# Seven half-size products in two chunks of the half-GLU, and merged rows added by transfers

## The chip, the cores and the metric

The kernel runs on one core of a Trainium2 chip. The core has a matrix engine (TensorE, in the profile PE for its matmuls and PEld for its weight loads), a vector engine (VectorE, DVE), an engine for activations (ScalarE, ACT), a general one (GpSimd, POOL) and one that here only issues transfers (SyncE, SP). They share an on-chip memory of 128 partitions (SBUF); matmuls write to a second, small one (PSUM). Each engine works through its own list of instructions in order and waits for others on semaphores. Transfers (DMA) are issued by SP, ACT or POOL, and those of one issuer form a queue.

The metric is the device time of one execution in microseconds (us). The kernel before takes 1742.87 us, the median of three executions from 1741.56 to 1743.77.

## The reference

One layer of a hybrid encoder, in fp32, applied to two requests of 256 and 512 tokens with the same weights. Three mixers (an S5 state-space model, differential attention, attention into memory tokens) work on the same projection of the input; then come the parts that this case is about:

```python
z = jax.nn.gelu(y)
s5_out = z * jax.nn.sigmoid(z @ s5_w_glu)                  # half-GLU
...
branches = jnp.stack([s5_out, diff_out, mem_out], axis=2)
br = jnp.einsum('blnc,ncd->blnd', branches, w_branch)      # three 1024 x 1024 products
gates = jax.nn.sigmoid(gl + b_gate)
merged = jnp.sum(gates * br, axis=2)
x = x + merged @ w_out
```

A feed-forward layer follows. z has 1024 channels for 768 tokens (both requests side by side); `s5_w_glu`, each `w_branch` and `w_out` are 1024×1024.

## The kernel before

**Products.** Activations lie with channels on partitions: eight rows of 128 channels × 768 tokens. An fp32 product is made of three matmuls of a shortened format (`mm3`): weights and activations are each split into a high and a low part, and high·high, high·low and low·high are added in PSUM. In the profile these are lines L755, L756 and L757. A 1024×1024 weight matrix is worked in four chunks of 256 columns. A chunk by the plain way takes, for each of two 128-column halves, eight k-steps of three matmuls over 256 tokens and three over 512: 96 matmuls.

**Seven products.** The last of the three branch products (`w_branch1`, function `branch7`) is made by a Strassen scheme with Winograd's sums. A chunk's weights are seen as four blocks: A11, A21 (the first 512 input channels, for the two output halves) and A12, A22 (the other 512). The activations are four blocks too: B11, B12 (first 512 channels, tokens 0–383 and 384–767) and B21, B22. Instead of eight block products there are seven: A11·B11, A12·B21, S1·T1, S2·T2, S3·T3, S4·B22 and A22·T4, with S1 to S4 sums of weight blocks and T1 to T4 differences of activation blocks. Each takes 4 k-steps × 3 = 12 matmuls over 384 tokens, so a chunk has 84. A11·B11, S2·T2 and S3·T3 add up in one PSUM tile (`chain`, name `brc`); after each of them ACT copies the tile out (c11, c12, c21: L1683, L1685, L1690) before the next may add to it. S4·B22 is added to S1·T1's tile (`p5`), which ACT has copied to c22 (L1687). DVE adds the other products to these quarters (`plus`, L1673).

**Weights** come through `WStream`: SP loads two tiles of 512 KB a chunk; for a plain chunk ACT makes the high part (L599) and DVE the low part (L605), each 128×1024. For a chunk of kind `w2`, POOL makes S1, S2, S3, S4 (L574, L575, L581, L583, in two buffers), and each of the seven factors, 128×512, is split by ACT (L557) and DVE (L558). The split tiles have four buffers, in which two factors share a tile.

**Order of the stages.** Branch 2 (memory attention), the half-GLU of the S5 branch in four plain chunks (L1590 to L1613), preparation of the T blocks for the last branch, branch 0 (S5), branch 1 by `branch7`, then `w_out`. The half-GLU computes, for a chunk, tanh of half the product (L1611), then (1+tanh)·z with z loaded again from its copy in DRAM by POOL's queue (`zs`, L1604), then splits the result into high and low (`s5o`, tiles S, lines L749 and L750). z itself stays split in the tiles Z (`zhi`, `zlo`).

**Merging** in `branch7`: a gate row comes from DRAM by POOL's queue (L1657), ACT turns it into tanh (L1658), DVE multiplies it with a result row `cs[m]` (L1677), the product is added to the row of `merged` (L1678; the chunk's first row by POOL, its second by DVE), and `merged` is split for `w_out` into MG (`mgd`: ACT L1679, DVE L1680).

**Buffers.** The pool `stg` has two buffers of 128×768, tag `brr`, which serve the reloaded z rows and, in `branch7`, the two result rows of a chunk (named `bs`). The gates and the GLU's results (`gt`) share two buffers of another pool. PSUM tiles of products have three buffers.

What sets the order on each engine is a planner: the program is written stage by stage, and a scheduler that simulates the engines orders every engine's list by when operands and buffers come free. So matmuls of the next chunk stand between those of the one before, and the written order is not the order run.

## Time and profile before

| | |
|---|---|
| median of three executions | 1742.87 us |
| profiled execution | 1743.06 us |
| its span (first to last instruction) | 1741.3 us |
| PE busy | 1726.6 us, 99% of the span |
| DVE, ACT, POOL busy | 1300.5, 908.6, 302.5 us |
| half-GLU, four chunks | from 987.07 to 1053.89 us |
| preparation and branch 0 | to 1120.74 us |
| last branch (`branch7`) | to 1183.75 us |

A row of the timeline has the start, the duration, the engine, the line, the operation, the tile written and the tiles read, and in brackets how long the engine had been idle before and what ended that. A row of groups has the count behind an x, the busy time, the mean nanoseconds of one, and idle time before them with its releasers. Matmuls overlap, so their pace is the distance between their starts. A row of transfers has the size and the median time from issue to landing.

### The profile page before, as it was taken

To read this page: it belongs to the slowest core of one execution; us is meant where nothing else is said; L and a number is where in the kernel's file an instruction comes from. 1 tells how busy PE (TensorE), PEld (TensorE's weight loads), DVE (VectorE), ACT (ScalarE), POOL (GpSimd) and SP (SyncE) were. 2 spreads that over 40 slices of the span, in tenths; PEclk is the share of its full clock that TensorE was granted. 3 is DMA by queue.
4 is the path that set the end of the run, shared out by engine and by line. 5 is a ranking of instruction groups with operands and counts; after the bars stand their busy time and mean duration, and the time that the engine had idled before them with its cause. 6 is when DMAs were issued, how large, how long until landed. Compare 5 with 4: busy or idle time off the path is not lost.

```text
span 1741.3 us, 29531 instructions
## 1 busy us (share of the span) xinstructions
PE 1726.6 (99%) x11188; PEld 1608.1 (92%) x11188; DVE 1300.5 (75%) x2405; ACT 908.6 (52%) x1924; POOL 302.5 (17%) x308
## 2 busy tenths in 40 slices
PE   9999999999999999999999999999999999999999
PEld 9999988999999999999989888998889999998887
DVE  7665749699999778887886536685598777776775
ACT  7444543776767346877765434353343333334443
POOL 0000000000000100111000001341036555541130
PEclk9999999999999999999999999999999999999999
DMA  7222636755556454745653435335312323239974
GB/s 268 78 85 91 125 120 135 186 125 143 145 159 159 115 140 103 164 91 156 155 165 117 140 116 157 103 111 174 97 55 91 110 91 109 92 110 295 248 157 97
DMA packets 209213, 234.09 MB, mean 134 GB/s; under 512 B 57832, under 2 KB 173296, under 8 KB 209072
## 3 DMA queue, kind: packets, MB, share of 16 engines
q1 hardware_dynamic: 182160, 167.49, 32.0%
q0 software_dynamic: 17440, 58.34, 15.6%
q10 hardware_dynamic: 9472, 6.39, 1.3%
q8 instruction: 88, 1.44, 0.4%
q14 instruction: 53, 0.43, 0.1%
HBM read 165.78 MB, written 41.22 MB: 119 GB/s over the span
## 4 chain that ended last, share of the span: by engine, by line
PE 95%; DVE 2%; ACT 1%; issue 0%; DMA 0%; POOL 0%; SPq 0%; ACTq 0%; DVEq 0%
PE gl L755 4%; PE gl L756 4%; PE gl L757 4%; PE gate L755 3%; PE gate L756 3%; PE up L756 3%; PE gate L757 3%; PE up L755 3%; PE up L757 3%; PE dn L757 3%; PE dn L755 3%; PE dn L756 3%; PE br L755 3%; PE br L757 3%; PE br L756 3%; PE qk L755 3%
## 5 line engine op out<-in xcount | busy, mean ns | idle before, releaser
L599 ACT ACTIVATE wh<-wr 128x1024 fp32r<-128x1024 f32 x116 | 131.9, 1138 | 52.3 <-PE br L756 13.3
L605 DVE TENSOR_TENSOR wl<-wr,wh 128x1024 fp32r<-128x1024 f32 x74 | 99.2, 1342 | 63.5 <-ACT wh L599 61.7
L755 PE MATMUL gl<-H,wh 128*128 128x256 f32 (+1 forms) x384 | 132.2, 344 | 0.0
L757 PE MATMUL gl<-H,wl 128*128 128x256 f32 (+1 forms) x384 | 129.0, 336 | 0.0
L756 PE MATMUL gl<-H,wh 128*128 128x256 f32 (+1 forms) x384 | 128.7, 335 | 0.0
L603 POOL DMA_DIRECT2D wl<-wr x42 | 36.6, 872 | 483.3 <-ACT wl L602 464.1
L755 PE MATMUL qk<-wh,H 128*128 128x256 f32 x384 | 108.3, 282 | 0.0
L756 PE MATMUL qk<-wl,H 128*128 128x256 f32 x384 | 108.0, 281 | 0.0
L757 PE MATMUL qk<-wh,H 128*128 128x256 f32 x384 | 107.3, 279 | 0.0
L558 DVE TENSOR_TENSOR wl_S<-ws,wh_S 128x512 fp32r<-128x512 f32 x84 | 70.7, 863 | 26.2 <-ACT wh_S L557 26.2
L756 PE MATMUL dn<-wld,dxh 128*128 128x512 f32 x231 | 89.6, 389 | 0.0
L755 PE MATMUL dn<-whd,dxh 128*128 128x512 f32 x231 | 89.5, 389 | 0.0
L757 PE MATMUL dn<-whd,dxl 128*128 128x512 f32 x231 | 88.9, 389 | 0.0
L557 ACT ACTIVATE wh_S<-ws 128x512 fp32r<-128x512 f32 x84 | 49.5, 625 | 73.5 <-PE up L756 36.6
L757 PEld LDWEIGHTS gl<-H,wl 128*128 128x128 f32 x384 | 72.0, 188 | 8.1
L756 PEld LDWEIGHTS gl<-H,wh 128*128 128x128 f32 x384 | 72.2, 188 | 7.2
L755 PEld LDWEIGHTS gl<-H,wh 128*128 128x128 f32 x384 | 72.3, 188 | 6.9
L757 PEld LDWEIGHTS qk<-wh,H 128*128 128x128 f32 x384 | 72.6, 189 | 0.6
L755 PEld LDWEIGHTS qk<-wh,H 128*128 128x128 f32 x384 | 72.4, 188 | 0.6
L756 PEld LDWEIGHTS qk<-wl,H 128*128 128x128 f32 x384 | 72.3, 188 | 0.5
L1296 DVE TENSOR_REDUCE nm<-sc 128x1 f32<-128x512 f32 (+1 forms) x96 | 56.7, 597 | 18.1 <-PE sc L1291 17.2
L1298 ACT ACTIVATE p<-sc,nm 128x512 f32<-128x512 f32 (+1 forms) x96 | 58.8, 615 | 14.4 <-DVE nm L1296 13.9
(535 smaller groups left out, 6076.2 us busy)
## 6 DMA issues: line engine op xcount, KB each, us to landing
wr<-in_w_in_dram SPq DMA_DIRECT2D x48, 512.0 KB, 5.0
wr<-in_w_gate_up_dram SPq DMA_DIRECT2D x44, 512.0 KB, 3.6
wl<-wr POOLq DMA_DIRECT2D x42, 512.0 KB, 5.4
wr<-in_w_branch_dram SPq DMA_DIRECT2D x24, 512.0 KB, 4.5
glr<-gl_scr POOLq DMA_DIRECT2D x24, 384.0 KB, 3.5
hid_scr<-fa SPq DMA_DIRECT2D x11, 768.0 KB, 6.4
wr<-in_w_mem_kv_dram SPq DMA_DIRECT2D x16, 512.0 KB, 4.4
wr<-in_w_in_dram SPq DMA_DIRECT2D x32, 256.0 KB, 3.9
```

The source lines that it names most:

```text
L557: self.nc.scalar.activation(f(hi), src, AF.Copy)
L558: self.nc.vector.tensor_tensor(out=f(lo), in0=src, in1=f(hi).bitcast(F32), op=ALU.subtract)
L599: self.nc.scalar.activation(hi, r, AF.Copy)
L603: self.nc.gpsimd.dma_start(lo, r.bitcast(F32R), accum_op=ALU.add)
L605: self.sub.tensor_tensor(out=lo, in0=r, in1=hi.bitcast(F32), op=ALU.subtract)
L755: pe.matmul(ps, wh, xh, start=start, stop=False, **kw)
L756: pe.matmul(ps, wh, xl, start=False, stop=False, **kw)
L757: pe.matmul(ps, wl, xh, start=False, stop=stop, **kw)
L1296: v.tensor_reduce(out=nm[:, m : m + 1], in_=ps, axis=AX.X, op=ALU.max, negate=True)
L1298: act.activation(pm[:, 0:n], ps, AF.Exp, bias=nm[:, m : m + 1], accum_out=s1s[:, tt : tt + 1] if m == 0 else s2)
```

## The change

**Half-GLU.** Chunks 2 and 3 are of kind `w2` and go through a new `glu7`, which makes the seven products with z's blocks. B11, B21 and B22 are slices of Z. T1, T2 and T3 are made by `z_differences`, once for each of the four k-rows while chunks 0 and 1 run: two z rows are loaded again by POOL's queue (into two slots of S that are still free), DVE makes four differences of 128×384, and ACT and DVE split them. T1 lies in S, T2 and T3 in a tile that is otherwise free (`zc`). T4's parts are made when chunk 2 begins, and overwrite Z's block B12, which chunks 2 and 3 don't read. This adds eight loads of 384 KB and, for two chunks, eight weight sums on POOL. POOL's two sum buffers are opened ahead of the half-GLU now. Results go to two tiles `gt` of 128×768 in quarters; tanh, the product with z and the split are done for a quarter at a time (`fin`).

**Last branch.** In chunks 0 to 2 the product of gate and result is added to `merged` by a transfer of POOL's queue that adds at its destination (`accum_op`), in place of the POOL and DVE additions; the split of these two rows into MG (`merged_parts`) stands in the next chunk. In chunk 3 both rows are added by DVE. S1·T1 is written third, ahead of S2·T2.

```diff
     for nme in ("w_branch2", "s5_w_glu", "w_branch0", "w_branch1"):
         for c in range(4):
-            W.add(cols(nme, 256 * c), 8, 256, "w2" if nme == "w_branch1" else None)
+            seven = nme == "w_branch1" or nme == "s5_w_glu" and c > 1
+            W.add(cols(nme, 256 * c), 8, 256, "w2" if seven else None)
...
+        def put(P, n_, k, src, scale=None):
+            split_evac(P[n_][0][:, k], P[n_][1][:, k], src, scale)
+        def prod(w, P, l, r, ps=None, start=True):
+            if ps is None:
+                ps = psd("p7")[:, 0:HT]
+            (wh, wl), (xh, xl) = w[l], P[r]
+            for k in range(4):
+                mm3(ps, wh[:, k], wl[:, k], xh[:, k], xl[:, k], start and k == 0, k == 3, not start)
+            return ps
+        def plus(o, ps):
+            v.tensor_tensor(out=o, in0=o, in1=ps, op=add)
+        def differences(P, k, r0, r1, t4):
+            (b11, b12), (b21, b22) = ((r[:, h1], r[:, h2]) for r in (r0, r1))
+            v.tensor_tensor(out=b11, in0=b12, in1=b11, op=sub)
+            v.tensor_tensor(out=b12, in0=b22, in1=b12, op=sub)
+            v.tensor_tensor(out=b22, in0=b22, in1=b11, op=sub)
+            v.tensor_tensor(out=t4, in0=b21, in1=b22, op=sub)
+            put(P, "T2", k, b22)
+            put(P, "T1", k, b11)
+            put(P, "T3", k, b12)
+        zc = xp.tile([128, 8, TOK], F32R, name="zc", tag="x1")
+        q = quarters(zc)
+        ZB = {"B11": tuple(x[:, 0:4, h1] for x in Z), "B21": tuple(x[:, 4:8, h1] for x in Z),
+              "B22": tuple(x[:, 4:8, h2] for x in Z), "T2": (q[0], q[1]), "T3": (q[2], q[3]),
+              "T1": tuple(halves(x[:, 6:8]) for x in S), "T4": tuple(x[:, 0:4, h2] for x in Z)}
+        zt4 = t4p.tile([128, 4, HT], F32, name="zt4", tag="t4")
+        def z_differences(k):
+            r0, r1 = (S[j][:, 4 + k % 2].bitcast(F32) for j in range(2))
+            gp.dma_start(r0, z_scr[k])
+            gp.dma_start(r1, z_scr[k + 4])
+            (b11, b12), (b21, b22) = ((r[:, h1], r[:, h2]) for r in (r0, r1))
+            d = stg.tile([128, TOK], F32, name=uid("zd"), tag="brr")
+            t1, t3 = d[:, h1], d[:, h2]
+            v.tensor_tensor(out=t1, in0=b12, in1=b11, op=sub)
+            v.tensor_tensor(out=t3, in0=b22, in1=b12, op=sub)
+            put(ZB, "T1", k, t1, 0.5)
+            put(ZB, "T3", k, t3, 0.5)
+            v.tensor_tensor(out=t1, in0=b22, in1=t1, op=sub)
+            v.tensor_tensor(out=zt4[:, k], in0=b21, in1=t1, op=sub)
+            put(ZB, "T2", k, t1, 0.5)
+        def z_row(M):
+            zs = stg.tile([128, TOK], F32, name=uid("zs"), tag="brr")
+            gp.dma_start(zs, z_scr[M])
+            return zs
+        def glu7(c):
+            w = W.get()
+            if c == 2:
+                for k in range(4):
+                    put(ZB, "T4", k, zt4[:, k], 0.5)
+            ts = [gtp.tile([128, TOK], F32, name=uid("gt"), tag="glr") for _ in range(2)]
+            zs = [z_row(2 * c + m) for m in range(2)]
+            (c11, c12), (c21, c22) = ((t[:, h1], t[:, h2]) for t in ts)
+            chain = env.psb("gluc")[:, 0:HT]
+            def fin(m, h):
+                t, M = ts[m][:, h], 2 * c + m
+                act.activation(t, t, AF.Tanh, scale=0.5)
+                v.scalar_tensor_tensor(out=t, in0=t, scalar=1.0, in1=zs[m][:, h], op0=add, op1=mul)
+                split_evac(S[0][:, M, h], S[1][:, M, h], t, 0.25)
+            act.activation(c11, prod(w, ZB, "A11", "B11", chain), AF.Copy)
+            plus(c11, prod(w, ZB, "A12", "B21"))
+            p5 = prod(w, ZB, "S1", "T1")
+            act.activation(c22, p5, AF.Copy)
+            act.activation(c12, prod(w, ZB, "S2", "T2", chain, False), AF.Copy)
+            fin(0, h1)
+            prod(w, ZB, "S3", "T3", chain, False)
+            plus(c22, chain)
+            act.activation(c21, chain, AF.Copy)
+            fin(1, h2)
+            plus(c12, prod(w, ZB, "S4", "B22", p5, False))
+            fin(0, h2)
+            plus(c21, prod(w, ZB, "A22", "T4"))
+            fin(1, h1)
...
+        for c in range(2):
...
+                z_differences(M)
+        for c in range(2, 4):
+            glu7(c)
+        t4 = t4p.tile([128, 4, HT], F32, name="t4", tag="t4")
...
+        def merged_parts(M):
+            act.activation(MG[0][:, M], merged[:, M], AF.Copy, scale=0.5)
+            v.scalar_tensor_tensor(out=MG[1][:, M], in0=merged[:, M], scalar=0.5,
+                                   in1=MG[0][:, M].bitcast(F32), op0=mul, op1=sub)
...
                 def merge(m):
                     M = 2 * c + m
                     v.scalar_tensor_tensor(out=cs[m], in0=gs[m], scalar=1.0, in1=cs[m], op0=add, op1=mul)
-                    (v if m else gp).tensor_tensor(out=merged[:, M], in0=merged[:, M], in1=cs[m], op=add)
-                    act.activation(MG[0][:, M], merged[:, M], AF.Copy, scale=0.5)
-                    v.scalar_tensor_tensor(out=MG[1][:, M], in0=merged[:, M], scalar=0.5,
-                                           in1=MG[0][:, M].bitcast(F32), op0=mul, op1=sub)
-
-                act.activation(c11, prod("A11", "B11", chain), AF.Copy)
-                plus(c11, prod("A12", "B21"))
-                act.activation(c12, prod("S2", "T2", chain, False), AF.Copy)
-                p5 = prod("S1", "T1")
+                    if c < 3:
+                        gp.dma_start(merged[:, M], cs[m], accum_op=add)
+                    else:
+                        v.tensor_tensor(out=merged[:, M], in0=merged[:, M], in1=cs[m], op=add)
+                        merged_parts(M)
+
+                act.activation(c11, prod(w, RB, "A11", "B11", chain), AF.Copy)
+                plus(c11, prod(w, RB, "A12", "B21"))
+                p5 = prod(w, RB, "S1", "T1")
                 act.activation(c22, p5, AF.Copy)
-                prod("S3", "T3", chain, False)
+                act.activation(c12, prod(w, RB, "S2", "T2", chain, False), AF.Copy)
+                prod(w, RB, "S3", "T3", chain, False)
                 plus(c22, chain)
                 act.activation(c21, chain, AF.Copy)
+                if c:
+                    for m in range(2):
+                        merged_parts(2 * c - 2 + m)
                 if c < 3:
-                    plus(c12, prod("S4", "B22", p5, False))
+                    plus(c12, prod(w, RB, "S4", "B22", p5, False))
                     merge(0)
-                    plus(c21, prod("A22", "T4"))
+                    plus(c21, prod(w, RB, "A22", "T4"))
                     merge(1)
                 else:
-                    plus(c21, prod("A22", "T4"))
+                    plus(c21, prod(w, RB, "A22", "T4"))
                     merge(1)
-                    plus(c12, prod("S4", "B22", p5, False))
+                    plus(c12, prod(w, RB, "S4", "B22", p5, False))
                     merge(0)
 
         branch7(1)
```

Line numbers in the changed kernel: `plus` L1611, `differences` L1613 to L1621, `z_differences` L1631 to L1644, `fin` L1663 to L1665, the copies of `glu7` L1667 (c11), L1670 (c22), L1671 (c12), L1675 (c21), `merged_parts` L1729 and L1730, gate loads L1742 and L1743, transfers that add L1753, the copies of `branch7` L1758 (c11), L1761 (c22), L1762 (c12), L1765 (c21). L749 and L750 have become L750 and L751.

How the planner orders it, at three places. The numbers behind the names tell buffers' uses apart.

ACT at the end of the half-GLU, before: the tanh rows of the last chunk (256 and 512 tokens, L1611), the split of s5o (L749), and branch 0's first weights (L599) and gate (L1518):

```order
L1611 ACTIVATE gt_12864<-glu_12867 128x256
L749 ACTIVATE s5o<-gt_12794 128x768
L1611 ACTIVATE gt_12864<-glu_12893 128x512
L749 ACTIVATE s5o<-gt_12864 128x768
L1611 ACTIVATE gt_12922<-glu_12925 128x256
L599 ACTIVATE wh_0_13070<-wr_0_12734 128x1024
L1518 ACTIVATE glr_13082<-glr_13082 128x768
```

ACT at the change from chunk 2 to chunk 3, now (`gluc_12850` is chunk 2's chain, `gluc_12980` chunk 3's):

```order
L557 ACTIVATE wh_S_12819<-ws_12809 128x512
L1671 ACTIVATE gt_12844<-gluc_12850 128x384
L557 ACTIVATE wh_S_12828<-ws_12810 128x512
L557 ACTIVATE wh_S_12828<-wr_1_12630 128x512
L1663 ACTIVATE gt_12844<-gt_12844 128x384
L557 ACTIVATE wh_S_12819<-ws_12823 128x512
L599 ACTIVATE wh_0_12962<-wr_0_12661 128x1024
L750 ACTIVATE s5o<-gt_12844 128x384
L1675 ACTIVATE gt_12845<-gluc_12850 128x384
L1663 ACTIVATE gt_12845<-gt_12845 128x384
L1667 ACTIVATE gt_12974<-gluc_12980 128x384
```

Four splits of chunk 3's factors, a tanh, branch 0's first weights and chunk 2's last copies stand ahead of c11 of chunk 3 (L1667), which writes a `gt` buffer that held chunk 2's first result row (`gt_12844`). The first split into `wh_S_12828` takes the buffer that chunk 2's S3·T3 reads last. On PE stand, in the meantime, chunk 3's S1·T1 and A22·T4 (24 matmuls); S2·T2 adds to the tile of c11 next. In chunk 2 PE has S1·T1 and S2·T2 k-step by k-step among 12 matmuls of A22·T4 and, pulled ahead, chunk 3's A11·B11 and A12·B21; chunk 2's own A11·B11 stands within chunk 0.

POOL in chunks 1 and 2 of the last branch, before (weight sums, the merged row's addition, gate loads):

```order
L583 TENSOR_TENSOR ws_13754<-wr_1_13596,ws_13754 128x512
L581 TENSOR_TENSOR ws_13765<-wr_0_13479 128x512
L1678 TENSOR_TENSOR merged<-merged,bs_13786 128x768
L574 TENSOR_TENSOR ws_13896<-wr_0_13625,wr_1_13747 128x512
L1657 DMA glr_13923<-gl_scr_152 128x768
L575 TENSOR_TENSOR ws_13897<-ws_13896,wr_0_13625 128x512
L1657 DMA glr_13926<-gl_scr_153 128x768
```

and now:

```order
L583 TENSOR_TENSOR ws_13856<-wr_1_13702,ws_13856 128x512
L581 TENSOR_TENSOR ws_13867<-wr_0_13585 128x512
L1753 DMA merged<-bs_13888 128x768
L1742 DMA glr_14025<-gl_scr_152 128x768
L574 TENSOR_TENSOR ws_13998<-wr_0_13731,wr_1_13849 128x512
L575 TENSOR_TENSOR ws_13999<-ws_13998,wr_0_13731 128x512
L1753 DMA merged<-bs_13889 128x768
L1742 DMA glr_14028<-gl_scr_153 128x768
```

The place of POOL's addition is taken by the issue of a transfer, a second one stands behind the sums L574 and L575, and the gate loads behind each.

ACT from chunk 2 to chunk 3 of the last branch, before (`brc_13931` is chunk 2's chain, `brc_14055` chunk 3's):

```order
L1690 ACTIVATE bs_13930<-brc_13931 128x384
L1679 ACTIVATE mgd<-merged 128x768
L1683 ACTIVATE bs_14053<-brc_14055 128x384
L1658 ACTIVATE glr_14047<-glr_14047 128x768
L599 ACTIVATE wh_1_14041<-wr_1_13892 128x1024
L1685 ACTIVATE bs_14053<-brc_14055 128x384
L1679 ACTIVATE mgd<-merged 128x768
L1687 ACTIVATE bs_14054<-br_14096 128x384
```

and now (`brc_14033` and `brc_14157`):

```order
L1765 ACTIVATE bs_14032<-brc_14033 128x384
L1758 ACTIVATE bs_14155<-brc_14157 128x384
L1729 ACTIVATE mgd<-merged 128x768
L1743 ACTIVATE glr_14149<-glr_14149 128x768
L599 ACTIVATE wh_1_14143<-wr_1_13994 128x1024
L1762 ACTIVATE bs_14155<-brc_14157 128x384
L1761 ACTIVATE bs_14156<-p_1514_14185 128x384
```

The copy of c11 (L1758) writes a buffer that the first transfer of chunk 2 reads, and the parts of the merged rows stand behind it. On PE, 30 matmuls stand between the end of chunk 2's S4·B22 and chunk 3's S2·T2; S3·T3 follows S2·T2 at once there, where before A22·T4 stood between them. In chunks 0 to 2 S1·T1 stood ahead of S2·T2 on PE before, too, and still does.

45 lines of the change are left out of this document (13 added, 32 removed).

## The prediction

> **What bounds the kernel now.** I read the page's busy times first, then its chain of waits, then the stretches of the stages that the change touches, then the single waits in them.
>
> ```profile
> span 1741.3 us, 29531 instructions
> PE 1726.6 (99%) x11188; PEld 1608.1 (92%) x11188; DVE 1300.5 (75%) x2405; ACT 908.6 (52%) x1924; POOL 302.5 (17%) x308
> PE 95%; DVE 2%; ACT 1%; issue 0%; DMA 0%; POOL 0%; SPq 0%; ACTq 0%; DVEq 0%
> ```
>
> TensorE (PE) is the bound, so a matmul less is time less, unless the work that feeds it comes late. The execution shown took 1743.06 us, 1.76 more than its span and 0.19 more than the median of 1742.87. My sum is made against 1743.06 and moved down by 0.19 at the end. Some 0.2% (3.5 us) is what a measurement of this kernel can tell from no change: faster is below 1739.4, slower above 1746.4.
>
> Stretches (columns: length, then busy time and instructions of each engine, PE's granted clock, DMA share, GB/s): the first, second and last of the four half-GLU chunks, branch 0, the last branch, and its undisturbed part.
>
> ```profile
> 987.07:1003.85 16.78, 16.78 (x97) 14.69 (x96) 9.73 (x12) 8.00 (x13) 2.69 (x5) 1.00 0.71 222
> 1003.85:1020.53 16.68, 16.68 (x97) 14.76 (x96) 7.81 (x8) 6.40 (x11) 1.61 (x3) 1.00 0.32 103
> 1037.21:1053.89 16.68, 16.68 (x97) 14.76 (x96) 6.20 (x6) 6.40 (x10) 1.61 (x3) 1.00 0.44 135
> 1053.89:1120.74 66.85, 66.85 (x386) 58.71 (x384) 46.73 (x82) 27.32 (x46) 14.81 (x19) 1.00 0.47 144
> 1120.74:1183.75 63.01, 60.56 (x337) 59.72 (x336) 51.49 (x62) 33.86 (x59) 26.93 (x22) 0.97 0.38 119
> 1120.74:1155.93 35.19, 35.19 (x204) 35.19 (x203) 27.09 (x36) 18.05 (x35) 16.91 (x13) 1.00 0.29 94
> ```
>
> The GLU chunks have no wait in PE, and VectorE (DVE) is busy half the time or less. In the undisturbed part 203 matmuls of 384 columns start in 35.19 us, one in 0.1733 us. At that pace the last branch's 336 would take 58.23, so 4.78 of its 63.01 are lost. The waits and the rows around them show where:
>
> ```profile
> PE brc L757 <- DVE wl_A L558: 2.1, 1, 2.1
> PE brc L755 <- ACT bs L1683: 0.3, 1, 0.3
> 1156.28 0.34 PE L756 MATMUL brc<-ra,wh_A 128*128 128x384 f32 x1
> 1158.74 0.44 PE L757 MATMUL brc<-ra,wl_A 128*128 128x384 f32 x1 [2.12 <-DVE wl_A L558]
> 1160.17 0.52 PE L755 MATMUL brc<-ra,wh_A 128*128 128x384 f32 x1
> 1160.49 0.52 PE L756 MATMUL brc<-ra,wh_A 128*128 128x384 f32 x1
> 1154.08 0.69 DVE L558 TENSOR_TENSOR wl_S<-ws,wh_S 128x512 fp32r<-128x512 f32 x1
> 1155.15 3.54 DVE L558 TENSOR_TENSOR wl_A<-wr,wh_A 128x512 fp32r<-128x512 f32 x2
> 1154.24 2.22 POOL L1678 TENSOR_TENSOR merged<-merged,bs 128x768 f32<-128x768 f32 x1 [2.34 <-DVE bs L1677]
> 1156.42 1.71 POOL L574 TENSOR_TENSOR ws<-wr,wr 128x512 f32<-128x512 f32 x1
> 1174.45 0.34 PE L757 MATMUL br<-rb,wl_S 128*128 128x384 f32 x1
> 1175.12 0.45 PE L755 MATMUL brc<-rc,wh_A 128*128 128x384 f32 x1 [0.33 <-ACT bs L1683]
> 900.10 1.16 PE L1327 MATMUL av<-V,aT 128*128 128x128 f32 x8 [1.21 <-ACT aT L1315]
> 900.10:907.00 6.90, 6.17 (x42) 5.16 (x42) 4.67 (x16) 5.65 (x21) 0.00 (x0) 1.00 0.09 33
> 1158.74:1163.10 4.36, 4.36 (x17) 4.36 (x18) 4.36 (x6) 1.41 (x2) 1.77 (x2) 0.63 0.59 201
> ```
>
> While POOL added a merged row (L1678) and then made a sum (L574), DVE's weight splits took 1.77 us each instead of 0.69. PE stood for 2.46−0.17 = 2.29, and then matmuls started 0.32 apart instead of 0.173 at half clock, about 12 of them: 1.8. Another 0.50 went at 1174.45. That is 4.6 of the 4.78. The wait of 1.21 at 900.10 left the clock at 1.00 over the next 6.9 us; the one of 2.12 did not.
>
> **The change part by part.** (1) Matmuls. A GLU chunk has 96 matmuls in 16.68; seven products have 84, at 0.1733 each 14.56. Two chunks: **−4.25**. Nothing else that PE does is added or removed.
>
> (2) What feeds the new products. The rows for the sizes:
>
> ```profile
> L747 DVE TENSOR_TENSOR mgd<-t,mgd 128x384 fp32r<-128x384 f32 x4 | 1.9, 545 | 0.0
> L605 DVE TENSOR_TENSOR wl<-wr,wh 128x1024 fp32r<-128x1024 f32 x4 | 5.4, 1355 | 1.5 <-ACT wh L599 1.5
> L599 ACT ACTIVATE wh<-wr 128x1024 fp32r<-128x1024 f32 x4 | 4.2, 1054 | 3.0 <-PE brc L756 2.7 <-PE br L756 0.3
> L557 ACT ACTIVATE wh_S<-ws 128x512 fp32r<-128x512 f32 x14 | 8.3, 622 | 8.3 <-POOL ws L581 5.4 <-PE brc L756 2.8
> L1683 ACT ACTIVATE bs<-brc 128x384 f32<-128x384 f32 x4 | 1.9, 470 | 0.0
> L1677 DVE SCALAR_TENSOR_TENSOR bs<-glr,bs 128x768 f32<-128x768 f32 x8 | 7.6, 950 | 0.1
> ```
>
> Each z difference set costs DVE four differences and three low parts of 128x384, 7×0.545 = 3.8, so 15.3 for four; T4's low parts 2.2; the first five factors of chunk 2 3.4 at 0.69. With the 9.73+7.81 that chunks 0 and 1 have already, DVE has 38.4 us of work before the last part of T1 is used. PE gives it both chunks (33.46), the products A11·B11 and A12·B21 of chunk 2 (4.16) and 30 matmuls more (5.2): 42.8. The margin of 4.4 is as large as what four POOL sums would cost if each slowed one split from 0.69 to 1.77 (4.3). The wait here is bounded by 0 and, with the second four sums as well, 4.3; I take **1.3**, nearer the covered end since sums and splits won't all meet. The eight extra z loads delay the weights and Z's last rows in chunk 0: **0.2**, bounded by 0 and 1.
>
> At the change-over to chunk 3, S2·T2 adds to a PSUM tile that ACT must first have emptied (c11), into a buffer that chunk 2's c12 frees. Behind the end of chunk 2's S3·T3 stand on ACT two splits of a factor, a tanh, another split, 3×0.62+0.47 = 2.33, the next weights' high part 1.05, then DVE's low part of them 1.36, a low part of the result 0.54, the evacuation 0.47: 5.75. PE has S1·T1 and A22·T4 to do meanwhile, 24×0.1733 = 4.16: **1.6** lost (0 if the order lets tanh be early, 3 if DVE is behind). S4·B22 and branch 0's first products, which need the last rows of s5o: **0.2**. GLU waits together 3.3; the last branch, which works the same way, lost 4.78 in four chunks or 2.4 in two, so 3.3 is on its dear side because DVE is fuller here. Sum of (1) and (2): −0.95.
>
> (3) The last branch. POOL loses three adds of 2.2 (below) and gets six issues of transfers of some 0.55; DVE loses three adds of 0.95. The contended wait at 1158.74 goes down by two splits that are now 1.1 instead of 1.77, to 0.9, too short by the row at 900.10 to cost the clock. What is late next is the landing: the buffers of c11 and c22 (two in all) come free only when the transfer has added them.
>
> ```profile
> L1678 POOL TENSOR_TENSOR merged<-merged,bs 128x768 f32<-128x768 f32 x4 | 8.9, 2216 | 15.4 <-DVE bs L1677 15.4
> L558 DVE TENSOR_TENSOR wl_A<-wr,wh_A 128x512 fp32r<-128x512 f32 x10 | 10.9, 1110 | 4.5 <-ACT wh_A L557 4.5
> L1678 DVE TENSOR_TENSOR merged<-merged,bs 128x768 f32<-128x768 f32 x4 | 3.8, 949 | 0.0
> 1171.97 1.84 POOL L1678 TENSOR_TENSOR merged<-merged,bs 128x768 f32<-128x768 f32 x1 [3.29 <-DVE bs L1677]
> L1657 POOL DMA_DIRECT2D glr<-gl_scr x8 | 4.4, 552 | 9.8 <-DVE bs L1677 7.0 <-DVE merged L1527 2.8
> L1679 ACT ACTIVATE mgd<-merged 128x768 fp32r<-128x768 f32 x7 | 5.9, 845 | 8.2 <-DVE merged L1678 6.6 <-POOL merged L1678 1.6
> L575 POOL TENSOR_TENSOR ws<-ws,wr 128x512 f32<-128x512 f32 x3 | 4.2, 1409 | 0.1
> L574 POOL TENSOR_TENSOR ws<-wr,wr 128x512 f32<-128x512 f32 x3 | 4.7, 1559 | 9.4 <-DVE wl_S L558 5.7 <-DMA wr<-in_w_branch_dram 3.7
> wl<-wr POOLq DMA_DIRECT2D x42, 512.0 KB, 5.4
> glr<-gl_scr POOLq DMA_DIRECT2D x24, 384.0 KB, 3.5
> ```
>
> No 384-KB transfer adds before. Its nearest rows are the adding transfer of 512 KB (5.4; by bytes 4.05) and the plain one of 384 KB (3.5): I take 3.8 between them and keep 3.5 and 6.4 (5.4 and 1.0 for traffic) for the range. In chunk 3 the path is c12's last add (0.545, by its size), the gate product 0.95, landing 3.8, evacuation 0.47: 5.77. Behind the end of chunk 2's S4·B22 PE has 30 matmuls, 5.20: 0.6 lost. Chunk 2's c22 waits for chunk 1's second add, which POOL issues behind two sums (1.56 and 1.41): 0.3. S2·T2 and S3·T3 stand side by side in chunk 3, so that the evacuation between them (0.33+0.47 and the hand-over, less 0.17) shows in full: 0.8. With the 0.9 above, 2.6 is lost instead of 4.78: **−2.2**. At 4.5 us of landing these become 1.3, 1.4 (c22, and the two behind it on ACT), 0.8 and 0.9, 4.4 in all, and the gain is gone.
>
> (4) S1·T1 third: on PE it stood ahead of S2·T2 already in three chunks of four, so 0. The parts of merged rows made a chunk later cost ACT and DVE the same, with PE's 84 matmuls of a chunk as cover; without it, 0.85 a row. Both last adds on DVE, 0.95 instead of POOL's 1.84 for one: 0 (±0.4).
>
> Sum: 1743.06 − 4.25 + 3.3 − 2.2 = 1739.9, against the median **1739.7**.
>
> [...]
>
> **The rivals.** *All covered* (0.30): DVE's margin holds and the change-over loses only its 0.7 or so: −4.25+1.0−2.2 gives 1737.4. For it speaks that chunks 0 and 1 lose nothing now; against it that DVE goes from half full to nine tenths.
>
> *Late adds* (0.20), slower: at 6.4 us of landing chunk 3's wait is 3.2, chunk 2's 2.8, and with 0.3, 0.9 and 0.8 that is 8.0; both long waits halve the clock like the one at 1158.74, 1.8 each. 11.6 against 4.78 is +6.8, and the time 1743.06−4.25+3.3+6.8−0.19 = 1748.7. It becomes slower than now from about 5.2 us. For it: the adding row's 5.4. Against: that row has a third more bytes.
>
> [...]
>
> *DVE as the bound of the GLU* (0.12), slower: the sums meet the splits and PE waits 4.3 in one go in chunk 2 and 3 at the change-over, both with the clock: 4.3+3+3.6+0.4 against 4.25, less 2.2: 1747.7. A wait over 2 us decides. *The change does not do its work* on PE's order (part 4) is certain for the product's place and is in the sum.
>
> **How the numbers follow.** My own case has 0.38, with 1737.5 to 1742; it lies across the bound of 1739.4, 0.15 of it below. Faster: 0.30 less 0.02, and 0.15: 0.43. Slower: 0.20 and 0.12 less 0.03 that stay under 1746.4: 0.29. The rest, 0.28, is the same. The range reaches from 1735.8 to 1748: its low end is no wait in the GLU and a landing of 3.5 (0.3, 0.9 and 0.8 lost, so 2.8 won: 1743.06−4.25−2.8−0.19), its high end lies just under the late adds.
>
> **What would show it.** Right: GLU chunks 2 and 3 last 14.6 us and their waits; one wait of 1 to 2 us on an evacuation of c11 into a gt tile; adds landing in 3.5 to 4.5; no L1678 of POOL; granted clock 1.00 at the last chunk of the branch. Wrong: waits on DVE's wl or T parts of more than 2 us with a clock near 0.6 behind them, or adds landing above 5.

## The result, and the profile after

The changed kernel takes 1749.83 us (median, 1748.75 to 1750.27); before it was 1742.87. The ratio is 1.004, with a 95% interval of 1.0028 to 1.0052: slower by 7 us, where 3 us less were forecast. The profiled execution has a span of 1747.8 us, 6.5 more than before.

The page of the changed kernel, with span, busy times and the chain of waits:

```profile
span 1747.8 us, 29638 instructions
PE 1725.0 (99%) x11164; PEld 1608.4 (92%) x11164; DVE 1325.2 (76%) x2461; ACT 923.2 (53%) x1962; POOL 319.4 (18%) x326
PE 93%; DVE 2%; DMA 2%; ACT 2%; issue 1%; POOL 0%; SPq 0%; ACTq 0%; POOLq 0%
```

PE is as busy as before, but the chain of waits now runs through transfers for 2% of the span, where before it was 0%. Two stretches tell where the time is: first the half-GLU with branch 0, then the last branch, of the kernel before and then of the changed one.

```profile
987.07:1120.74 133.67, 133.67 (x770) 117.69 (x768) 76.66 (x113) 53.66 (x84) 21.80 (x32) 1.00 0.46 143
```

```profile
986.72:1120.28 133.56, 130.20 (x745) 117.33 (x744) 109.16 (x172) 67.40 (x122) 41.47 (x49) 1.00 0.52 167
1120.28:1189.81 69.53, 61.83 (x337) 59.53 (x336) 44.73 (x59) 34.03 (x58) 27.39 (x29) 0.98 0.54 144
```

The half-GLU's 24 matmuls less bring 0.1 us. The last branch, 63.01 before, takes 69.53, 6.5 more, which is the whole loss; 11.3 of it are above the 58.23 that its 336 matmuls take at their undisturbed pace. PE's own waits over both stretches (in total, times, longest):

```profile
PE brc L756 <- ACT bs L1762: 2.4, 1, 2.4
PE brc L756 <- ACT bs L1758: 2.3, 2, 1.9
PE p L756 <- ACT bs L1761: 1.9, 2, 1.0
PE p L756 <- DVE gt L1611: 1.7, 1, 1.7
PE br L756 <- DVE glr L1525: 1.6, 1, 1.6
PE p L756 <- DVE bs L1611: 1.1, 2, 0.9
```

The first three are copies of PSUM tiles by ACT in the last branch: c12, c11, c22. ACT's timeline from chunk 2's last copy on, with POOL's issues and PE's two long waits, shows what the copies stood behind:

```profile
1173.67 0.88 POOL L1753 DMA_DIRECT2D merged<-bs  x1 [3.98 <-DVE bs L1751]
1174.74 0.56 POOL L1742 DMA_DIRECT2D glr<-gl_scr  x1 [0.19 <-issue]
...
1171.94 0.49 ACT L1765 ACTIVATE bs<-brc 128x384 f32<-128x384 f32 x1 [0.53 <-DVE bs L1611]
1178.71 0.49 ACT L1758 ACTIVATE bs<-brc 128x384 f32<-128x384 f32 x1 [6.28 <-DMA merged<-bs]
1179.10 0.84 ACT L1729 ACTIVATE mgd<-merged 128x768 fp32r<-128x768 f32 x1
1181.75 0.84 ACT L1743 ACTIVATE glr<-glr 128x768 f32<-128x768 f32 x1 [1.81 <-DMA glr<-gl_scr]
1182.50 1.04 ACT L599 ACTIVATE wh<-wr 128x1024 fp32r<-128x1024 f32 x1
1183.44 0.47 ACT L1762 ACTIVATE bs<-brc 128x384 f32<-128x384 f32 x1
...
1179.26 0.44 PE L756 MATMUL brc<-rc,wh_A 128*128 128x384 f32 x1 [1.88 <-ACT bs L1758]
1183.97 0.44 PE L756 MATMUL brc<-rc,wh_S 128*128 128x384 f32 x1 [2.36 <-ACT bs L1762]
```

The add issued at 1173.67 has landed at 1178.7. Until then ACT cannot copy c11 into the buffer that the add reads, and PE stands until 1179.26. Then the gate load of 1174.74, in the same queue, has to land (1181.7) before ACT can do the gate's tanh, and c12's copy stands behind that tanh and a weight split, for which PE stands until 1183.97. Behind this second wait the granted clock is 0.52 from 1184.65 to 1188.05. The medians of both transfers, the gate loads of all three branches together:

```profile
merged<-bs POOLq DMA_DIRECT2D x6, 384.0 KB, 4.6
glr<-gl_scr POOLq DMA_DIRECT2D x24, 384.0 KB, 4.8
```

An add takes 4.6 (4.3 to 7.3), inside the range of 3.5 to 6.4 and 0.8 over the value taken. The gate loads' median went from 3.5 to 4.8. For the eight of the last branch alone, most of which now stand behind an add, it went from 3.4 to 6.1.

### The profile page after: what moved, and what is told of

Its sections match the earlier page's. It is cut to its first block, busy times and chain, and to the rows that moved or that the text cites. A ratio compares the mean times of both kernels' runs of the same rounds, so it can differ in the third digit from the quotient of the medians.

```text
span 1747.8 us, 29638 instructions
## 1 busy us (share of the span) xinstructions
PE 1725.0 (99%) x11164; PEld 1608.4 (92%) x11164; DVE 1325.2 (76%) x2461; ACT 923.2 (53%) x1962; POOL 319.4 (18%) x326
## 4 chain that ended last, share of the span: by engine, by line
PE 93%; DVE 2%; DMA 2%; ACT 2%; issue 1%; POOL 0%; SPq 0%; ACTq 0%; POOLq 0%
PE gl L756 4%; PE gl L758 4%; PE gl L757 4%; PE gate L756 3%; PE gate L758 3%; PE up L756 3%; PE up L758 3%; PE gate L757 3%; PE up L757 3%; PE dn L758 3%; PE dn L757 3%; PE dn L756 3%; PE qk L756 3%; PE qk L758 3%; PE qk L757 3%; PE br L756 2%
## 5 line engine op out<-in xcount | busy, mean ns | idle before, releaser
L599 ACT ACTIVATE wh<-wr 128x1024 fp32r<-128x1024 f32 x112 | 127.7, 1141 | 44.8 <-PE br L757 13.7
L605 DVE TENSOR_TENSOR wl<-wr,wh 128x1024 fp32r<-128x1024 f32 x70 | 93.8, 1342 | 51.0 <-ACT wh L599 49.1
L558 DVE TENSOR_TENSOR wl_S<-ws,wh_S 128x512 fp32r<-128x512 f32 x91 | 75.0, 844 | 28.2 <-ACT wh_S L557 28.2
L557 ACT ACTIVATE wh_S<-ws 128x512 fp32r<-128x512 f32 x91 | 53.8, 626 | 73.5 <-PE up L757 36.6
```

The source lines that it names most:

```text
L557: self.nc.scalar.activation(f(hi), src, AF.Copy)
L558: self.nc.vector.tensor_tensor(out=f(lo), in0=src, in1=f(hi).bitcast(F32), op=ALU.subtract)
L599: self.nc.scalar.activation(hi, r, AF.Copy)
L605: self.sub.tensor_tensor(out=lo, in0=r, in1=hi.bitcast(F32), op=ALU.subtract)
```

## The experiments

Each ratio is against the kernel before on the same chip, with a 95% interval; that kernel takes 1741.8 to 1742.9 us from chip to chip, so ratios compare better than times. The two right columns are the stretches as above, from one profile each. The eleven kernels with the same half-GLU as the changed one (all but `before`, `adds_only`, `b_dve`, `ts_dve` and those named `pre_`) have 132.4 to 133.8 in the first of them, so differences within that spread tell nothing.

| kernel | time, us | ratio | half-GLU and branch 0 | last branch |
|---|---|---|---|---|
| before | 1742.87 | 1 | 133.67 | 63.01 |
| as changed | 1749.83 | 1.0040 (1.0028 to 1.0052) | 133.56 | 69.53 |
| glu_only | 1742.02 | 1.0001 (0.9991 to 1.0010) | 133.10 | 62.48 |
| adds_only | 1746.34 | 1.0028 (1.0019 to 1.0038) | 133.47 | 67.71 |
| no_third | 1748.35 | 1.0035 (1.0024 to 1.0047) | 132.46 | 68.91 |
| four_bufs | 1751.59 | 1.0056 (1.0041 to 1.0071) | 133.41 | 71.50 |
| sp_gates | 1754.85 | 1.0069 (1.0054 to 1.0084) | 133.56 | 73.19 |
| four_sp_late | 1752.14 | 1.0052 (1.0035 to 1.0069) | 133.03 | 72.36 |
| dve_add | 1741.50 | 0.9992 (0.9983 to 1.0001) | 132.86 | 62.31 |
| unwaited | 1742.01 | 0.9992 (0.9983 to 1.0002) | 133.78 | 61.06 |
| b_dve | 1740.99 | 0.9989 (0.9980 to 0.9999) | 133.47 | 61.02 |
| behind2 | 1759.41 | 1.0095 (1.0079 to 1.0111) | 133.05 | 78.49 |
| behind4 | 1747.16 | 1.0031 (1.0020 to 1.0041) | 132.43 | 67.30 |
| behind4b | 1744.94 | 1.0015 (1.0006 to 1.0024) | 133.07 | 64.34 |
| ts_dve | 1743.00 | 1.0003 (0.9994 to 1.0013) | 133.88 | 61.07 |
| pre_dve | 1741.40 | 0.9989 (0.9979 to 0.9999) | 130.84 | 64.64 |
| pre_pool | 1743.05 | 1.0001 (0.9992 to 1.0011) | 130.80 | 66.03 |
| pre_dve_behind | 1746.15 | 1.0023 (1.0014 to 1.0032) | 130.25 | 67.25 |
| pre_dve_g0 | 1738.58 | 0.9978 (0.9969 to 0.9987) | 131.27 | 62.58 |

### One part at a time

`glu_only` undoes the last branch's part:

```diff
-                    if c < 3:
-                        gp.dma_start(merged[:, M], cs[m], accum_op=add)
-                    else:
-                        v.tensor_tensor(out=merged[:, M], in0=merged[:, M], in1=cs[m], op=add)
-                        merged_parts(M)
+                    (v if m else gp).tensor_tensor(out=merged[:, M], in0=merged[:, M], in1=cs[m], op=add)
+                    merged_parts(M)
...
-                if c:
-                    for m in range(2):
-                        merged_parts(2 * c - 2 + m)
```

The place of S1·T1 goes back too.

> Seven products in the half-GLU alone; the last branch adds its rows by POOL and DVE, in the old product order. Theory (the transfers that add are the whole loss): the last branch takes 63 to 64 us as before, the half-GLU with branch 0 the 133.6 of the changed kernel (133.7 before), so 1742 to 1743.5. Rival (the GLU's new work delays what follows): the last branch stays above 66, 1746 or more.

1742.02, at the time before. The last branch is back at 62.48, the half-GLU with branch 0 is 0.6 shorter, within the spread. The GLU's part does no harm, and any good is too small to tell.

`adds_only` is the kernel before with that diff turned round (and the parts of a row a chunk later).

> The kernel before with only the transfers that add (chunks 0 to 2), the later split of merged rows and DVE's two adds in chunk 3; half-GLU plain, product order as before. Theory: the last branch goes from 63.0 to 69 or 70 us and the time to 1748.5 to 1750. Rival (it takes the GLU's changes or the third place of S1*T1 as well): under 66 and under 1746.

1746.34, 4.5 us over before on that chip (1748.5 to 1750 was expected): the adds alone do most of it. The last branch takes 67.71, 4.7 more than before (69 or 70 was expected), and ACT waits as in the changed kernel:

```profile
1176.33 0.49 ACT L1689 ACTIVATE bs<-brc 128x384 f32<-128x384 f32 x1 [6.29 <-DMA merged<-bs]
1179.05 0.84 ACT L1663 ACTIVATE glr<-glr 128x768 f32<-128x768 f32 x1 [1.50 <-DMA glr<-gl_scr]
```

`no_third` writes S1·T1 behind S2·T2 again:

```diff
-                p5 = prod(w, RB, "S1", "T1")
-                act.activation(c22, p5, AF.Copy)
                 act.activation(c12, prod(w, RB, "S2", "T2", chain, False), AF.Copy)
+                p5 = prod(w, RB, "S1", "T1")
+                act.activation(c22, p5, AF.Copy)
```

> The changed kernel with S1*T1 written after S2*T2 again. Theory (the place of the product does not matter, the landing of the adds does): 1748.5 to 1751, as changed. Rival (S3*T3 right behind S2*T2 in chunk 3 costs its evacuation): 1 to 2.5 us less than changed.

1.0035 against 1.0040, with intervals that overlap widely, and the waits on c12's copy (2.4) and on c11's (1.9) are there as before: the place of the product is not the cause. The time alone, 1748.35, is 1.5 us under the changed kernel's, but most of that is the chip.

### What about the adds costs the time

Four result buffers, so that no copy waits for the add of the chunk before:

```diff
-                cs = [stg.tile([128, TOK], F32, name=uid("bs"), tag="brr") for _ in range(2)]
+                if c % 2:
+                    ct = t4p.tile([128, 2, TOK], F32, name=uid("bs"), tag="t4")
+                    cs = [ct[:, m] for m in range(2)]
+                else:
+                    cs = [stg.tile([128, TOK], F32, name=uid("bs"), tag="brr") for _ in range(2)]
```

> The changed kernel, but the result rows of chunks 1 and 3 of the last branch lie in a tile that is free by then (the raw T4), so there are four buffers in place of two, and no result waits for the landing of the chunk before. Theory (landing holds the buffers): ACT's 6.3 us wait ahead of c11 of chunk 3 and the PE waits behind it go, the last branch falls from 69.5 to about 65, the time to 1745 or 1746; what is left is the gate load that stands behind the adds in POOL's queue. Rival (the adds delay the branch by their queue or traffic and not by the buffers): above 1748.

The last branch got longer, 71.50. The time is above 1748, as the rival said, but the theories were both wrong as put: the waits of the copies on the adds went. Instead the high parts of merged rows (L1729), which wait for the same landings, stand on ACT in front of c22's and c12's copies, in chunk 3 further ahead than as changed, and wait there:

```profile
1159.27 0.85 ACT L1729 ACTIVATE mgd<-merged 128x768 fp32r<-128x768 f32 x1 [3.40 <-DMA merged<-bs]
1160.88 0.84 ACT L1743 ACTIVATE glr<-glr 128x768 f32<-128x768 f32 x1 [0.76 <-DMA glr<-gl_scr]
```

`sp_gates` loads the last branch's gates by SP (`nc.sync.dma_start` for `gp.dma_start`).

> The changed kernel with the gate loads of the last branch on SP's queue, so that they do not stand behind the transfers that add. Theory (ACT's list waits in order for landings, and the gate loads land late behind the adds): the PE wait of 2.5 us on c12's copy in chunk 3 shrinks below 1, the one of 2.0 on c11 stays, the last branch takes 66 to 67.5 us, 2 to 3 less than as changed. Rival (only the result buffers matter): no change within 1 us of the changed kernel.

73.19. In chunk 3 the planner now put a gate's tanh ahead of c11's copy; ACT waited 6.1 us for a gate and then 2.2 for the add, and PE 4.8 for c11. `four_sp_late` joins both and splits the merged rows two chunks after their add.

> The changed kernel with all that ACT waits for made early: four result buffers as in four_bufs, gate loads on SP's queue, and the merged rows split two chunks after their add instead of one (the last two at the end). The adds are still transfers. Theory (not the adds' own traffic but ACT's waiting for their landing costs the time): the last branch comes down to 62 to 64.5 us, the time to within 2 us of before. Rival (the transfers load SBUF or the queues so that splits and weights are slow): 67 us or more, and 4 us or more over before.

72.36: again parts and gates stand ahead of copies. Written order did not hold them back. So three attempts to ease a wait each made the last branch longer, and the numbers alone would have spoken for the rival, that transfers disturb by being there. The next two settle that.

`dve_add` has no transfers that add; DVE adds both rows, in all four chunks, and splits them in the same chunk again. `unwaited` is that, and six transfers of the same size that add, from the finished merged row into a dead tile (against `dve_add`):

```diff
                     v.tensor_tensor(out=merged[:, M], in0=merged[:, M], in1=cs[m], op=add)
+                    if c < 3:
+                        gp.dma_start(t4[:, 2 * m : 2 * m + 2].rearrange("p a t -> p (a t)"), merged[:, M], accum_op=add)
                     merged_parts(M)
```

> Seven products in the half-GLU and S1*T1 third, with both merged rows of every chunk added by DVE, none by POOL or a transfer. Theory (the 2.1 us wait of the kernel before came from POOL's add meeting DVE's weight splits): that wait and the half clock behind it go, the last branch takes 60 to 61.5 us, 1 to 2.5 less than with POOL's add, at or just under the time before. Rival (DVE is then too full): 63 us or more.

> As dve_add (both merged rows added by DVE), and in chunks 0 to 2 the same six transfers of 384 KB that add, issued at the same place of POOL's queue, but from the finished merged row into a dead tile: nothing waits for their landing, and the output does not depend on them. Theory (waiting for the landing of the adds costs the time, and the gate loads behind them a part): 0 to 3 us more than dve_add. Rival (queue, issue and traffic of the adds alone do it): 5 us or more over dve_add, at the time of the changed kernel.

`unwaited` is at 0.9992, as `dve_add`. Its adds move the same bytes and land no faster (4.9 against 4.6 in the median), yet the last branch is shorter than before:

```profile
1122.20:1183.26 61.06, 58.96 (x337) 57.99 (x335) 51.07 (x65) 33.79 (x59) 29.83 (x28) 1.00 0.59 154
...
t<-merged POOLq DMA_DIRECT2D x6, 384.0 KB, 4.9
```

So issue and traffic of the adds cost nothing that these runs can tell, and what costs time is waiting, for an add or for a gate load behind it. Which of the two, `unwaited` does not tell, since there only one of the six gate loads of chunks 1 to 3 is issued less than 3 us behind an add. `dve_add` did not lose its wait on wl_A, as had been expected; that is taken up below.

Then the order on ACT was forced: gates and merged parts behind the copy of c21 (in chunk 3 of `behind2` and `behind4`, behind that of c12). `issue_after` keeps a row behind the one named in its engine's list.

```diff
-                    act.activation(g, g, AF.Tanh, scale=0.5)
...
-                act.activation(c21, chain, AF.Copy)
-                if c:
-                    for m in range(2):
-                        merged_parts(2 * c - 2 + m)
+                i21 = act.activation(c21, chain, AF.Copy)
+                with tc.issue_after((i21 if c < 3 else i12).ins):
+                    for g in gs:
+                        act.activation(g, g, AF.Tanh, scale=0.5)
+                    if c:
+                        for m in range(2):
+                            merged_parts(2 * c - 2 + m)
```

> The changed kernel with one order forced on ACT in the last branch: in each chunk the tanh of the gates and the high parts of merged rows stand behind the copy of c21 (in chunk 3 behind that of c12), so that of ACT's copies out of PSUM only those wait for a landing whose result buffer is still being read. Theory (ACT's order is the larger part, the buffers the rest): the PE wait of 2.5 us on c12 in chunk 3 goes, that of 2.0 on c11 stays, and the last branch falls from 69.5 to 64 to 66.5 us. Rival (the buffers are all of it): 68 or more.

78.49, the slowest of all. With later gates the results are finished and added later, and the two buffers hold c11 up more: ACT waits 3.8 and 4.6 for adds ahead of two of its copies, and PE 9.8 us for these copies, 4.9 at the longest.

```profile
1165.73 0.49 ACT L1757 ACTIVATE bs<-brc 128x384 f32<-128x384 f32 x1 [3.82 <-DMA merged<-bs]
1185.96 0.49 ACT L1757 ACTIVATE bs<-brc 128x384 f32<-128x384 f32 x1 [4.56 <-DMA merged<-bs]
```

`behind4` is `behind2` with the four buffers of `four_bufs`.

> As behind2, with four result buffers as in four_bufs, so that no copy out of PSUM waits for a landing. Theory: no PE wait on an ACT copy above 0.5 us is left, the last branch takes 61 to 63 us, and the time is at that of dve_add (1741.5) within 2 us, though the six transfers that add are all there. Rival (the transfers disturb in another way): 65 us or more.

The branch's own waits are gone but for 0.9, and one of 7.5 stands at its end, where `w_out` needs the PSUM tile that c21's copy (L1768) empties. PE's waits from the start of that branch:

```profile
PE wo L756 <- ACT bs L1768: 7.5, 1, 7.5
PE p L756 <- ACT bs L1764: 0.7, 1, 0.7
PE p L756 <- DVE bs L1611: 0.2, 1, 0.2
```

In chunk 3 the gates and parts were held behind c12's copy alone, and on ACT they stand ahead of c21's, with two weight splits and a part that waits for DVE's last add. The branch takes 67.30, where 61 to 63 was expected; 67.30−7.5 leaves 59.8 for products that took 69.5 as changed. `behind4b` forces them behind c21's copy in chunk 3 too.

> As behind4, with the gates and merged parts of chunk 3 forced behind the copy of c21 too, so that no copy out of PSUM stands behind an instruction that waits for a transfer. Theory: the wait of 7.5 us at w_out falls to 1 to 4 (the last rows are then late), and the time from 1747.2 to 1741 to 1744. Rival (the landing costs what it costs, wherever ACT waits for it): 1746 or more.

A ratio of 1.0015 against 1.0040, some 4 us less than as changed, with all six adds still transfers. The wait at `w_out` is 4.8 (1 to 4 was expected) and comes from another load: a split of `w_out`'s weights (L599) waits for their landing in front of c21's copy. The time is 0.9 past the range expected. The rest of the branch takes 59.5, as short as in `behind4`, and the wait that is left is of the same kind, a row that waits for a transfer ahead of a copy. Why that load is late is not shown.

```profile
1181.65 1.06 ACT L599 ACTIVATE wh<-wr 128x1024 fp32r<-128x1024 f32 x1 [4.41 <-DMA wr<-in_w_out_dram]
1182.61 0.47 ACT L1768 ACTIVATE bs<-brc 128x384 f32<-128x384 f32 x1
```

### POOL's add and the wait on wl_A

`b_dve` is the kernel before with `v` in place of `(v if m else gp)`.

> The kernel before with both merged rows of the last branch added by DVE. Theory (POOL's weight sums hold up the splits): PE's wait of 2.1 us at the change to chunk 2 stays between 1.5 and 2.5, and the time is within 1.5 us of before. Rival (POOL's add holds them up): the wait falls under 1 us and the last branch from 63.0 to under 60.5.

The wait stays, 2.0 (as in `dve_add`), so POOL's add is not needed for it. POOL's weight sums are what is left beside DVE there. In `dve_add`, where POOL had no other work, the two splits of wl_A took 1.72 us each; in `b_dve` the two sums run from 1152.71 to 1156.3, and beside them a gate product (L1677) took 2.05 instead of 0.95 and the splits 1.2 each:

```profile
1155.23 3.44 DVE L558 TENSOR_TENSOR wl_A<-wr,wh_A 128x512 fp32r<-128x512 f32 x2
...
1154.67 1.79 POOL L574 TENSOR_TENSOR ws<-wr,wr 128x512 f32<-128x512 f32 x1 [3.52 <-DMA wr<-in_w_branch_dram]
1156.54 1.59 POOL L575 TENSOR_TENSOR ws<-ws,wr 128x512 f32<-128x512 f32 x1
...
PE brc L757 <- DVE wl_A L558: 2.0, 1, 2.0
1155.12 2.35 DVE L558 TENSOR_TENSOR wl_A<-wr,wh_A 128x512 fp32r<-128x512 f32 x2
```

The first three rows are of `dve_add`, the others of `b_dve`. In the changed kernel POOL's sums begin only at 1157.03, and the same two splits, from 1155.89, take 0.64 each. No run takes the sums away, so that they are the cause is argued from these overlaps.

`b_dve` is 2 us shorter in the last branch, mostly since the clock stays whole behind the wait in its profile (a mean of 1.00 over the branch, 0.97 before); its time is 1.8 under before, where 1.5 at most was expected, and its ratio, 0.9989, lies at the edge of what can be told.

### The half-GLU's own waits

The two waits that took its gain, as changed:

```profile
1043.26 0.44 PE L756 MATMUL p<-zhi,wh_S 128*128 128x384 f32 x1 [1.71 <-DVE gt L1611]
1064.67 0.50 PE L756 MATMUL br<-s5o,wh 128*128 128x512 f32 x1 [1.64 <-DVE glr L1525]
...
1041.06 1.21 DVE L605 TENSOR_TENSOR wl<-wr,wh 128x1024 fp32r<-128x1024 f32 x1
1042.19 0.54 DVE L751 SCALAR_TENSOR_TENSOR s5o<-gt,s5o 128x384 fp32r<-128x384 f32 x1
1042.66 0.54 DVE L1611 TENSOR_TENSOR gt<-gt,p 128x384 f32<-128x384 f32 x1
1056.47 0.54 POOL L1518 DMA_DIRECT2D glr<-gl_scr  x1 [1.80 <-DVE s5o L751]
1062.26 0.84 ACT L1519 ACTIVATE glr<-glr 128x768 f32<-128x768 f32 x1 [1.06 <-DMA glr<-gl_scr]
1063.17 0.56 DVE L1617 TENSOR_TENSOR brr<-brr,brr 128x384 f32<-128x384 f32 x1 [1.37 <-DMA brr<-br_scr]
1064.20 0.41 DVE L1525 SCALAR_TENSOR_TENSOR glr<-glr,br 128x256 f32<-128x256 f32 x1
```

At the change to chunk 3 PE waits for a PSUM tile that DVE empties (L1611), behind weights of branch 0 and a split. At branch 0 it waits for a tile that DVE empties with a gate (L1525). The gate came late, its tanh ending at 1063.1, since its load waited until the half-GLU's results were out of the shared buffers. But two rows of the preparation (L1617 and a split) stand ahead of L1525 on DVE too, and the first of them waited until 1063.17 for a load of its own, so the gate is not the only cause. `ts_dve` gives chunk 3's results a tile of their own (`t4p`), on top of `dve_add`.

> As dve_add, and chunk 3 of the half-GLU writes its results to a tile of its own (the raw T4, free there) instead of the two gate buffers, so that neither its c11 nor the gate loads of branch 0 wait for chunk 2's results or chunk 3's. Theory: the PE waits of 1.9 at the change to chunk 3 and of 0.5 to 1.9 at branch 0 shrink together by 2 us or more against dve_add. Rival (the first is a PSUM tile that DVE frees late behind other work): the first stays, under 1.5 us gained.

The first wait goes, and one of 2.05 at branch 0's start takes its place, behind which the matmuls of 512 columns start 0.34 and 0.32 apart instead of 0.23: the z rows of chunk 3 now landed too late, and DVE stood 2.37 for one. The time does not fall. `pre_dve` also loads those z rows into the gate buffers and branch 0's first two gates into the staging buffers:

```diff
+            if c == 3:
+                tt = t4p.tile([128, 2, TOK], F32, name=uid("gt"), tag="t4")
+                ts = [tt[:, m] for m in range(2)]
+                zs = [z_row(2 * c + m, gtp, "glr") for m in range(2)]
...
+        pre = []
+        for m in range(2):
+            g = stg.tile([128, TOK], F32, name=uid("glr"), tag="brr")
+            gp.dma_start(g, gl_scr[m])
+            act.activation(g, g, AF.Tanh, scale=0.5)
+            pre.append(g)
...
```

> As dve_add, with the buffers of the half-GLU's last chunk taken apart: its results lie in the raw-T4 tile, its z rows in the gate buffers, and branch 0's first two gates in the two buffers of the staging pool, ahead of the preparation of the last branch. Theory: the PE waits of 1.9 at the change to chunk 3 and of 1.6 at branch 0 are waits on shared buffers and go; 3 to 4 us less than dve_add, 1737 to 1739.5 where before has 1742.5. Rival (another late row takes their place, as in ts_dve): within 1.5 us of dve_add.

> As pre_dve, with POOL adding the first row of a chunk as in the kernel before. Theory (POOL's weight sums, which stay, hold up DVE's splits at the change to chunk 2 of the last branch, not POOL's add): PE's wait of about 2 us there stays as in dve_add, and the time is within 1.5 us of pre_dve, more where the wait falls so that the clock halves behind it. Rival (POOL's add is what holds them up): 2 us or more over pre_dve.

The half-GLU with branch 0 comes down to 130.8, 2.8 under before, and most of that goes back at once at the start of the last branch, in a wait of 2.3, where a gate's tanh that waits for its load stands ahead of c22's copy:

```profile
PE p L756 <- ACT bs L1771: 2.3, 1, 2.3
1129.51 0.84 ACT L1756 ACTIVATE glr<-glr 128x768 f32<-128x768 f32 x1 [3.88 <-DMA glr<-gl_scr]
```

So `pre_dve` stays near `dve_add`, as its rival had it. `pre_pool` has 66.03 in the last branch at a mean clock of 0.97, where `pre_dve` has 64.64 at 1.00; it is 1.65 us over `pre_dve`, between the 1.5 of its theory and the 2 of its rival, so it does not tell clearly. The attempt to mend that in all chunks at once, `pre_dve_behind`, fell short for the reason of `behind4`:

> As pre_dve, with the gates' tanh of the last branch forced behind the copy of c21 (of c12 in chunk 3). Theory (a gate's tanh that waits for its load ahead of c22's copy made PE's wait of 2.5 us at 1130.8): that wait goes, and the time falls from 1741.4 to 1738.5 to 1739.5, the first clearly under before (1742.8). Rival (another row takes its place): no more than 1 us gained.

It made the first wait go, and late gates made three others (2.1, 1.5 and 3.0). `pre_dve_g0` forces the two gates of chunk 0 alone behind c12's copy:

```diff
...
-                act.activation(c12, prod(w, RB, "S2", "T2", chain, False), AF.Copy)
+                i12 = act.activation(c12, prod(w, RB, "S2", "T2", chain, False), AF.Copy)
+                if c == 0:
+                    with tc.issue_after(i12.ins):
+                        for g in gs:
+                            act.activation(g, g, AF.Tanh, scale=0.5)
```

> As pre_dve, with the two gates of chunk 0 of the last branch alone forced behind the copy of c12. Theory: PE's wait of 2.5 us at the start of that branch goes and no other comes, 1738.5 to 1739.5 with before at 1742. Rival (another wait takes its place): above 1740.5.

1738.58 us, a ratio of 0.9978 (0.9969 to 0.9987): 3.7 us less than before on that chip, and faster than both kernels of this case. Not all of it is the seven products' doing. `b_dve`, with the plain half-GLU and DVE's adds, is at 0.9989 already, and the half-GLU with branch 0 is 2.4 shorter here than before. So the seven products pay some 2 us once their waits are gone; that is read from one profile's stretch, and the intervals of the two ratios just overlap. Its two stretches:

```profile
986.15:1117.42 131.27, 130.43 (x746) 117.41 (x745) 109.71 (x172) 66.74 (x121) 43.26 (x49) 1.00 0.52 170
1117.42:1180.00 62.58, 60.53 (x337) 59.57 (x335) 49.06 (x63) 34.42 (x60) 23.78 (x22) 0.97 0.38 120
```

## Why the prediction was wrong

**Part (1), −4.25,** was right in the pace: twelve matmuls of 384 columns in the half-GLU took 2.08 us, 0.173 each (1037.23 to 1039.31). Of the gain `pre_dve` gets 2.8 once most of the waits are gone.

**Part (2), +3.3,** came out at about +4.1 (−4.25 became −0.1). The change-over lost 1.9 against 1.6, in the place named but by another resource, a PSUM tile behind DVE's list. The 1.3 for DVE's margin in chunk 2 did not come: DVE was busy for 109 of 134 us, and the view shows no wait of PE there. What failed is the 0.2 for branch 0's first products, 1.8 measured: I priced the last rows of s5o and neither the gate load that waits for the same two buffers nor the preparation's rows ahead on DVE.

**Part (3), −2.2,** is the step that made the prediction wrong: +6.5 measured. It has 2.6 lost in the last branch where 11.3 were; PE's waits there add up to 7.7, and the half clock is 1.7 more. It has three errors. The landing was taken at 3.8, by bytes and a plain transfer, and is 4.6; in chunk 3 the add of c11's buffer took 5.0. With 5.0 the formula for c11 gives 1.8, and 2.0 was measured, so that term was mis-sized only by its landing. But at 4.5 of landing the prediction's own sum is 4.4 lost, 1.8 more than 2.6, so the landing explains a small part. Missing from the sum was the gate load behind the add in POOL's queue, with its tanh ahead of a split and c12's copy on ACT: a wait of 2.4, and the 1.7 for the clock, granted at 0.52 for 3.4 us behind it. The order on ACT showed that row ahead of the copy; I counted one waiting instruction and not what waits in the same list. And the wait on wl_A was to fall to 0.9 without POOL's add; `b_dve` and `dve_add` show that taking that add away does not shorten it. In the changed kernel the wait is not there at all, with POOL's sums behind those splits, so that this 0.9 erred on the dear side.

**Part (4), 0,** was right for the place of the product (`no_third`). That the parts a chunk later cost nothing was not tried by itself.

**The rivals.** "Late adds", to which I gave 0.20, had the direction and the kind of wait, and its numbers are near: 11.6 lost by its sum, 11.3 measured, 1748.7 forecast and 1749.83 measured. That they are so near is luck. Its condition, a landing of 6.4, did not come (4.6 in the median, though the slowest add took 7.3), and its parts differ: c11 2.0 instead of 3.2, c22 1.9 in two waits instead of 2.8, one half clock instead of two, and what it lacks is made up by the gate, which it did not have. "DVE as the bound of the GLU" fell. The range ended at 1748, below the time that this rival itself gave, so that it did not take in its price.

What is shown: the adds bring most of the loss (`adds_only`), their traffic does not (`unwaited`), and with the order forced and four buffers the waits inside the branch go (`behind4b`). What stays open is how the 6.5 us divide between the buffers that the adds hold and the gate loads behind them. `behind2` shows that the buffers are enough to hold c11 up, the changed kernel's c12 that a gate is; neither was taken away alone without another wait coming in its place.

## What to carry to other kernels

An engine that empties PSUM for TensorE should have nothing in its in-order list ahead of those copies that waits for a transfer: moving 2.2 us of arithmetic on POOL (L1678 before) into a transfer of 4.6 us can delay whatever stands behind the first reader of its result, and the loads behind it in its queue. Where a planner orders the lists, look at each waiting row in its order, and force the copies first. Here it took a forced order and more buffers together; forced order alone (`behind2`), more buffers alone (`four_bufs`) or another queue alone (`sp_gates`) made the branch longer. Price an asynchronous step by its landing in the place where it runs (here 4.6 in the median, 7.3 at most) and by all that is queued behind it, its buffers, readers and later loads, before its issue cost is called a gain.

## What the hardware showed that was not expected

A wait does not halve the clock by its length alone. With the wait of 2.0 us on wl_A the mean clock of the last branch is 1.00 in `dve_add`, `unwaited` and `b_dve`, and 0.97 in `pre_dve_g0` (the stretch above); it is 0.97 too with the 2.1 of the kernel before and the 1.8 of `glu_only`. In the kernel before, the clock behind that wait is 0.50 from 1160.00 to 1163.00. Behind the wait of 7.5 in `behind4` the matmuls of 512 columns start 0.43 apart from 1188.11 to 1189.81; behind the 4.8 in `behind4b` they do so until 1187.14, 4.0 us after the wait, and are 0.23 apart from 1187.42 on. The 1.8 us that the prediction put behind each wait of over 2 us is so a chance and not a price. What decides it is not shown.
